# A decoder layer's compressed-value product, made from float32r parts instead of float32

## The chip, the cores and the metric

The kernel runs on one core of a Trainium2 chip. The metric is the device time of one execution, in microseconds (us); the median of the runs counts. Engines are named as in the profile: PE is the matrix engine (TensorE), PEld its weight load, DVE is VectorE, ACT is ScalarE, POOL is GpSimd, SP is the queue that issues most DMAs.

## The reference, cut to what matters

The layer takes 512 tokens of width 2048, makes one input projection, runs two mixers on it (a sparse attention and a gated spatial mixer), merges them, projects back and adds a gated per-layer embedding. The change touches one of the three branches of the attention: the compressed one. There, keys and values are compressed to 31 blocks for each of 4 groups, each group has 4 heads, and per query block:

```python
sc = jnp.einsum('bqgrd,bngd->bgrqn', qb, kc).astype(jnp.float32) * scale
sc = jnp.where(vc_mask, sc - slopes[:, :, None, None] * dc.astype(jnp.float32), NEG)
p_c = jax.nn.softmax(sc, axis=-1) * vc_mask
o_c = jnp.einsum('bgrqn,bngd->bqgrd', p_c.astype(vc.dtype), vc)
...
o = (gb[:, :, 0, :, :, None] * o_c + gb[:, :, 1, :, :, None] * o_s +
     gb[:, :, 2, :, :, None] * o_w)
```

The edited product is `o_c`: probabilities over compressed blocks (in the kernel already weighted by their gate) times compressed values. Everything is float32.

## The kernel before, in words

**Parts.** Nearly all large products are made of float32r parts. A float32 operand is split into a high part, rounded to float32r by a copy on ACT (`high`, line 141), and a low part, the remainder, made by a subtraction on DVE (`low`, line 147; with a scale, lines 143 and 149). A product is then three matmuls: high by high, high by low, low by high. The low part is often put off with `deferred`: a list of functions that `flush()` runs ahead of the next piece of PE work.

**Order.** The order of instructions is written out by hand. `gemm()` is a generator that yields after each small set of matmuls of the dense projections (lines 337 to 339 are those that run beside the attention: `ps_q` for queries, `ps_za` for the gate path); `fill(n)` advances it by n pieces. The attention phase, some 200 to 490 us in the profile, is a loop over 48 slots, six for each `ft`, a pair of heads. In each slot it issues events: `scores` (lines 999 and 1000, two heads), `weigh`, `transpose_probs` (line 1051), `values` (lines 1070 and 1071) and, at fixed slots, the pieces of the compressed branch. Behind each event that uses PE it runs `fill` for a share of the dense work.

**The compressed branch**, once for each of 4 groups g (each serves `ft` = 2g and 2g+1):
- `cmp_scores` (line 1103): eight float32r matmuls for four heads, 32 rows a head.
- `cmp_softmax`, `cmp_weigh`: transposes back to tokens, softmax pieces on DVE, ACT and POOL.
- `cmp_transpose` (lines 1142 to 1148): four transposes into one bank `ps_c`, so that the rows are 4 heads by 32 blocks and the columns are the 512 tokens; one copy on ACT takes the bank to the float32 tile `pct` (line 1144). POOL writes the values of the group into `vcb`, [128, 2, 128]: index 0 holds heads 0 and 1 in rows 0 to 63, index 1 heads 2 and 3 in rows 64 to 127, zeros elsewhere.
- `cmp_values(ft)` (line 1152): one float32 matmul, `vcb[:, ft % 2]` by `pct`. Half of the rows of the weights are zeros: they cancel the two heads that belong to the other `ft`. A copy on ACT brings the result to `oc` (line 1154).

For group 0 the first four pieces run ahead of the loop. For the later groups `cmp_transpose` comes in the fifth slot of `ft` = 2g, and `cmp_values` in the sixth slot of the even and the fourth of the odd `ft`.

**Banks.** The results of PE go to banks of 128 rows by 512 columns. Those of kind "s" are two, given out in turn (`bank("s", ...)`); scores of the two heads of a slot (`ps_s`) and all `ps_c` share them. A bank is given out again when all its readers are done. The tiles of the pool `att` work in the same way; each tag has as many slots as its `bufs`, and `pct`, `ct` and `oc` have one each.

Of the kernel before, what the change touches and what calls it, by code (L numbers as in the profile page):

```python
# [13 lines left out]
F32 = mybir.dt.float32  # L14
F32R = mybir.dt.float32r
BF16 = mybir.dt.bfloat16
AF = mybir.ActivationFunctionType
ALU = mybir.AluOpType
# [3 lines left out]
P = 128  # L22
S = 512
# [5 lines left out]
HD = 64  # L29
# [34 lines left out]
def kernel(ctx: ExitStack, tc: tile.TileContext, x, p, norm_g, w_in,  # L64
                      pe_k, w1_k, w2_k, pe_v, w1_v, w2_v, ln_g, ln_b, sgu_w, sgu_b,
                      w_up_a, w_up_b, w_out, w_ple, w_ple_gate, final_g, out):
    nc = tc.nc
    x, out = x[0], out[0]
    p = p[0, 0]
# [10 lines left out]
    def bank(kind, name):  # L80
        return psum.tile([P, 512], F32, tag=kind, name=name)
# [49 lines left out]
    deferred = []  # L131
# [7 lines left out]
    def high(hi, src, scale=None):  # L139
        if scale is None:  # L140
            nc.scalar.copy(hi, src)  # L141
        else:
            nc.scalar.mul(hi, src, scale)

    def low(hi, lo, src, scale=None):
        if scale is None:
            nc.vector.tensor_tensor(out=lo, in0=src, in1=hi.bitcast(F32), op=ALU.subtract)  # L147
        else:
            nc.vector.scalar_tensor_tensor(out=lo, in0=src, scalar=scale, in1=hi.bitcast(F32),
                                           op0=ALU.mult, op1=ALU.subtract)  # L150
# [639 lines left out]
    with tc.tile_pool(name="xin", bufs=4, side="right") as xin:  # L790
# [43 lines left out]
        for j in range(2):  # L834
            b = bank("t", "ps_p")
# [6 lines left out]
        b = bank("o", "ps_g")  # L842
# [41 lines left out]
    vc = mid.tile([P, GROUPS, HD], F32, name="vc")  # L884
# [18 lines left out]
    with tc.tile_pool(name="cmp", bufs=1) as cmp:  # L903
# [17 lines left out]
        for n in range(2):  # L921
            b = bank("t", "ps_pe")
# [25 lines left out]
        t = o32[:, 4, 128:256].rearrange("p (g n) -> p g n", g=GROUPS)  # L948
        h = o32[:, 5].rearrange("p (g r n) -> p g r n", g=GROUPS, r=4)
        c = cmp.tile([P, 1], F32, name="hid_c")  # L950
# [12 lines left out]
        b = bank("o", "ps_kc")  # L963
        nc.tensor.matmul(b[:, :128], w2t[lo_r].rearrange("e i f -> e (i f)"), h[lo_r, :, 0], start=True, stop=True)
        split(kc_h, kc_l, b[:, :128].rearrange("p (g n) -> p g n", g=GROUPS))
        b = bank("o", "ps_vc")
        for g in range(GROUPS):
            nc.tensor.matmul(b[:, g * HD:g * HD + HD], h[up_r, g].rearrange("e r n -> e (r n)"), w2t[up_r, 0],
                             start=True, stop=True)
# [5 lines left out]
    att = ph_b.enter_context(tc.tile_pool(name="att", bufs=1))  # L975
    tmp_pool.update(p=att, n=1)
    kcp = att.tile([P, 2, 224], F32R, name="kcp")
    vcb = att.tile([P, 2, P], F32, name="vcb")
    nc.gpsimd.memset(kcp.bitcast(F32), 0.0)
    nc.gpsimd.memset(vcb, 0.0)  # L980

    slots = []
    for ft in range(8):
# [1 line left out]
    prob, obank, oc_t, pct_t = {}, {}, {}, {}  # L985
# [152 lines left out]
    def cmp_transpose(g):  # L1138
        c, _ = pct_t["c"]
        b = bank("s", "ps_c")  # L1140
        for i in range(TT):
            nc.tensor.transpose(b[:, i * P:i * P + P], c[:, i].rearrange("p r n -> p (r n)"), ident)
        t = att.tile([P, S], F32, tag="pct", name="pct")
        nc.scalar.copy(t, b)
        pct_t["p"] = t
        for r in range(4):
            nc.gpsimd.tensor_copy(vcb[32 * r:32 * r + 32, r // 2, (r % 2) * HD:(r % 2) * HD + HD],
                                  vc[32 * r:32 * r + 32, g])

    def cmp_values(ft):  # L1150
        b = bank("s", "ps_c")
        nc.tensor.matmul(b, vcb[:, ft % 2], pct_t["p"], start=True, stop=True)
        t = att.tile([P, S], F32, tag="oc", name="oc")
        nc.scalar.copy(t, b)
        oc_t[ft] = t
# [3 lines left out]
    for f, u in zip((cmp_scores, cmp_softmax, cmp_weigh, cmp_transpose), (4, 3, 4, 8)):  # L1159
        fill(u)  # L1160
        flush()
        f(0)
    n = len(slots)
    credit, per_period = 0.0, (phase_b_units - 19) / (n + 3)
    for s in range(n + 3):
        events = []
        if s < n:
            ft, j = slots[s][0], s % 6
            events.append((scores, s))
        if 1 <= s <= n:  # L1170
            events.append((weigh, s - 1))
        tq = [(transpose_probs, s - 2, bi) for bi in range(len(blocks(s - 2)))] if 2 <= s <= n + 1 else []
        vq = [(values, s - 3, bi) for bi in range(len(blocks(s - 3)))] if s >= 3 else []
        events += tq[:1] + vq[:1]
        if s < n:
            if ft % 2 == 1 and ft < 7 and j == 3:
                events.append((cmp_keys, (ft + 1) // 2))
            if ft % 2 == 1 and ft < 7 and j == 5:
                events.append((cmp_scores, (ft + 1) // 2))
            if ft % 2 == 0 and ft > 0 and j in (1, 2, 4):  # L1180
                events.append(({1: cmp_softmax, 2: cmp_weigh, 4: cmp_transpose}[j], ft // 2))
            if j == (3 if ft % 2 else 5):
                events.append((cmp_values, ft))
        events += tq[1:] + vq[1:]
        share = per_period / sum(e[0] not in off_pe for e in events)
        for e in events:
            if e[0] not in off_pe:
                flush()
            e[0](*e[1:])
            if e[0] not in off_pe:  # L1190
                credit += share
                fill(int(credit))
                credit -= int(credit)
# [134 lines left out]
    b = bank("s", "ps_b")  # L1328
# [3 lines left out]
    for hf in range(2):  # L1332
        b = bank("s", "ps_w")
        for j in range(4):
            nc.tensor.transpose(b[:, j * P:j * P + P], wn[hf][:, j], ident)
        nc.vector.tensor_tensor(out=ws[hf], in0=b.rearrange("p (g t) -> p g t", g=4),
                                in1=tri.unsqueeze(1).to_broadcast([P, 4, P]), op=ALU.mult)
# [386 lines left out]
```

## Time and profile before

| | |
|---|---|
| median of 3 runs | 1564.4 us (1564.28 to 1564.46) |
| profiled execution | 1564.27 us |
| its span | 1562.6 us |
| PE busy | 1548.0 us, 99% of the span |
| DVE busy | 1162.8 us, 74% |
| ACT busy | 772.7 us, 49% |
| POOL busy | 223.8 us, 14% |
| `cmp_values` matmuls (line 1152) | 16 records for 8 calls, 591 ns each, from 245.4 to 465.7 us |
| copies `pct` (line 1144) | 4, 576 ns each, at 220.0, 309.0, 375.6 and 441.1 us |

The span is the time from the first to the last instruction in the trace; the execution's own time lies a little above it. A row of the timeline gives start, duration, engine, line, operation, output and inputs, and in brackets for how long the engine stood idle before and what released it. Matmuls are pipelined: one starts before the one ahead has ended, so the distance between starts is what one costs.

### The profile page before, as it was taken

Reading aid. Unit: us, or ns where it says so; the run is one execution under the profiler, and the core shown is the slowest. Engines: PE = TensorE matmul, PEld = TensorE weight load, DVE = VectorE, ACT = ScalarE, POOL = GpSimd, SP = SyncE. Lnnn points to the kernel's source line nnn. Section 1 sums busy time; section 2 is a strip of 40 time slices with the busy share of each in tenths; the row PEclk is TensorE's granted clock in tenths of the full one; section 3 lists DMA queues with packets and bytes.
Section 4 is the critical chain, followed back from the end, with each engine's and each line's share of the span. In section 5 each row is a group of like instructions: output and inputs, shape, how many; then the busy total and the mean of one; then the engine's idle time right before and its main releaser. Section 6 shows DMA issues by size and latency. Waiting matters only on the chain.

```text
span 1562.6 us, 20467 instructions
## 1 busy us (share of the span) xinstructions
PE 1548.0 (99%) x7486; PEld 1296.4 (83%) x7486; DVE 1162.8 (74%) x1851; ACT 772.7 (49%) x1337; POOL 223.8 (14%) x348
## 2 busy tenths in 40 slices
PE   9999999999999999999999999999999999999997
PEld 8889988888888888888888888888888888888885
DVE  6543358888886977878887777777656587888877
ACT  6433346667664544454544444444423343544556
POOL 1200000101022520101121211220122221000000
PEclk9999999999999999999999999999999999999999
DMA  9423421112123993617473736675742387464654
GB/s 325 123 81 87 114 78 45 51 45 55 41 55 109 288 293 93 215 54 242 134 265 103 270 100 243 208 261 208 262 156 84 125 259 246 148 201 164 188 206 185
DMA packets 158213, 250.35 MB, mean 160 GB/s; under 512 B 8713, under 2 KB 82081, under 8 KB 156065
## 3 DMA queue, kind: packets, MB, share of 16 engines
q1 hardware_dynamic: 116224, 150.10, 31.0%
q0 software_dynamic: 41744, 98.69, 19.0%
q8 instruction: 59, 0.97, 0.3%
q14 instruction: 42, 0.34, 0.1%
q10 hardware_dynamic: 144, 0.26, 0.0%
HBM read 199.21 MB, written 49.81 MB: 159 GB/s over the span
## 4 chain that ended last, share of the span: by engine, by line
PE 96%; DVE 2%; ACT 1%; issue 0%; POOL 0%; DVEq 0%; POOLq 0%; ACTq 0%
PE ps_m L311 7%; PE ps_m L313 7%; PE ps_m L312 7%; PE ps_za L337 2%; PE ps_za L339 2%; PE ps_t L1051 2%; PE ps_za L338 2%; PE ps_u L349 2%; PE ps_u L350 2%; PE ps_ub L351 2%; PE ps_wo L349 2%; PE ps_ub L349 2%; PE ps_ub L350 2%; PE ps_wo L350 2%; PE ps_wo L351 2%; PE ps_u L351 2%
## 5 line engine op out<-in xcount | busy, mean ns | idle before, releaser
L147 DVE TENSOR_TENSOR ls<-b,hs 128x1024 fp32r<-128x1024 f32 x180 | 220.2, 1224 | 119.3 <-ACT hs L141 118.4
L141 ACT CAST hs<-b 128x1024 fp32r<-128x1024 f32 x180 | 189.2, 1052 | 213.4 <-PE ps_m L313 86.1
L147 DVE TENSOR_TENSOR lo<-raw,hi 128x512 fp32r<-128x512 f32 (+1 forms) x248 | 173.0, 703 | 111.3 <-issue 27.2
L141 ACT CAST hi<-raw 128x512 fp32r<-128x512 f32 (+1 forms) x248 | 149.5, 608 | 187.9 <-PE ps_ub L351 46.4
L141 ACT CAST hs<-raw 128x1024 fp32r<-128x1024 f32 x72 | 75.8, 1053 | 88.8 <-PE ps_m L313 35.8
L147 DVE TENSOR_TENSOR ls<-raw,hs 128x1024 fp32r<-128x1024 f32 x72 | 88.0, 1222 | 16.8 <-ACT hs L141 16.7
L311 PE MATMUL ps_m<-hs,act_h 128*128 128x512 f32 x256 | 100.5, 393 | 0.0
L312 PE MATMUL ps_m<-ls,act_h 128*128 128x512 f32 x256 | 99.7, 389 | 0.0
L313 PE MATMUL ps_m<-hs,act_l 128*128 128x512 f32 x256 | 99.7, 389 | 0.0
L240 DVE TENSOR_TENSOR b<-b,b 128x1024 f32<-128x1024 f32 x72 | 87.7, 1218 | 0.0
L240 DVE TENSOR_TENSOR b<-raw,b 128x1024 f32<-128x1024 f32 x72 | 87.6, 1217 | 0.0
L141 ACT CAST pth<-ps_t 128x512 fp32r<-128x512 f32 (+1 forms) x88 | 47.9, 545 | 65.7 <-PE ps_t L1051 65.4
L1012 ACT ACTIVATE prob<-prob,st 128x512 f32<-128x512 f32 (+3 forms) x128 | 70.6, 555 | 4.0 <-DVE st L1003 3.8
L147 DVE TENSOR_TENSOR ptl<-ps_t,pth 128x512 fp32r<-128x512 f32 (+1 forms) x88 | 56.2, 638 | 21.1 <-ACT pth L141 20.3
L1003 DVE CUSTOM_DVE_ANT_0 prob<-ps_s,b 128x512 f32<-128x512 f32 (+3 forms) x128 | 56.3, 486 | 10.1 <-PE ps_s L1000 9.9
L313 PEld LDWEIGHTS ps_m<-hs,act_l 128*128 128x128 f32 x256 | 48.0, 188 | 10.1
L311 PEld LDWEIGHTS ps_m<-hs,act_h 128*128 128x128 f32 x256 | 48.1, 188 | 9.7
L312 PEld LDWEIGHTS ps_m<-ls,act_h 128*128 128x128 f32 x256 | 48.1, 188 | 9.7
L337 PE MATMUL ps_za<-act_h,hi 128*128 128x512 f32 x128 | 55.8, 436 | 0.0
L337 PE MATMUL ps_q<-act_h,hi 128*128 128x512 f32 x128 | 53.6, 419 | 0.0
L1051 PEld LDWEIGHTS ps_t<-ident,prob 128*128 128x128 f32 x320 | 39.7, 140 | 13.9 <-DVE ptl L147 2.8
L1051 PE MATMUL ps_t<-ident,prob 128*128 128x128 f32 x320 | 49.5, 273 | 1.3 <-DVE ptl L147 1.2
(590 smaller groups left out, 4374.3 us busy)
## 6 DMA issues: line engine op xcount, KB each, us to landing
raw<-in_w_in_dram SPq DMA_DIRECT2D x116, 512.0 KB, 3.9
b<-in_w_in_dram SPq DMA_DIRECT2D x48, 512.0 KB, 5.4
raw<-in_w_out_dram SPq DMA_DIRECT2D x24, 512.0 KB, 4.7
raw<-in_w_ple_gate_dram SPq DMA_DIRECT2D x24, 512.0 KB, 4.1
raw<-in_w_up_b_dram SPq DMA_DIRECT2D x16, 512.0 KB, 3.9
oa_d<-oa POOLq DMA_DIRECT2D x28, 256.0 KB, 4.7
gate<-keep POOLq DMA_DIRECT2D x24, 256.0 KB, 3.7
xt<-in_x_dram SPq DMA_DIRECT2D x4, 1024.0 KB, 10.3
```

Source lines behind the costliest of these rows:

```text
L141: nc.scalar.copy(hi, src)
L147: nc.vector.tensor_tensor(out=lo, in0=src, in1=hi.bitcast(F32), op=ALU.subtract)
L240: nc.vector.tensor_tensor(out=b[o], in0=b[x], in1=b[y], op=ALU.subtract)
L311: nc.tensor.matmul(o, ah, hi[:, i], start=st, stop=False, skip_group_check=go)
L312: nc.tensor.matmul(o, ah, lo[:, i], start=False, stop=False, skip_group_check=go)
L313: nc.tensor.matmul(o, al, hi[:, i], start=False, stop=sp, skip_group_check=go)
L337: nc.tensor.matmul(ps, hi[:, j], ah, start=st, stop=False)
L349: nc.tensor.matmul(o, ah[:, sl], hi[:, j], start=st, stop=False)
L350: nc.tensor.matmul(o, ah[:, sl], lo[:, j], start=False, stop=False)
L351: nc.tensor.matmul(o, al[:, sl], hi[:, j], start=False, stop=sp)
L1012: nc.scalar.activation(sl, sl, AF.Exp, bias=st[:, 0, j, hh:hh + 1], scale=-1.0, accum_out=st[:, 1, j, hh:hh + 1])
L1051: nc.tensor.transpose(b[:, (2 * e + hh) * P:(2 * e + hh + 1) * P], pts[hh][:, c:c + P], ident)
```

## The change

`vcb` and the probabilities become float32r. `vcb` index 0 now holds the high parts of the values for all four heads, index 1 their low parts. The probabilities are kept in two tiles, one for each `ft` of the group: in the tile for the even `ft`, rows 0 to 63 hold the high parts of heads 0 and 1, and rows 64 to 127, which met zeros before, hold the low parts of the same two heads; in the tile for the odd `ft` it is the other way round, for heads 2 and 3. A matmul by index 0 so gives high values times (high + low) probabilities, and one by index 1 low values times the same; both add up in one bank.

The copy of the bank on ACT becomes two copies of 64 rows each. Two subtractions of 64 rows on DVE, which read the bank and the high parts, are put in `deferred`. POOL makes a subtraction behind each of its four copies into `vcb`. The second tile takes the slot `ct`. Each fp32 matmul of `cmp_values` becomes two float32r matmuls.

```diff
-    vcb = att.tile([P, 2, P], F32, name="vcb")
+    vcb = att.tile([P, 2, P], F32R, name="vcb")
     nc.gpsimd.memset(kcp.bitcast(F32), 0.0)
-    nc.gpsimd.memset(vcb, 0.0)
+    nc.gpsimd.memset(vcb.bitcast(F32), 0.0)
...
         for i in range(TT):
             nc.tensor.transpose(b[:, i * P:i * P + P], c[:, i].rearrange("p r n -> p (r n)"), ident)
-        t = att.tile([P, S], F32, tag="pct", name="pct")
-        nc.scalar.copy(t, b)
-        pct_t["p"] = t
+        rows = slice(0, 64), slice(64, 128)
+        pct_t["p"] = [att.tile([P, S], F32R, tag=tag, name="p" + tag) for tag in ("pct", "ct")]
+        for e, t in enumerate(pct_t["p"]):
+            high(t[rows[e]], b[rows[e]])
+
+        def lows():
+            for e, t in enumerate(pct_t["p"]):
+                low(t[rows[e]], t[rows[1 - e]], b[rows[e]])
+        deferred.append(lows)
         for r in range(4):
-            nc.gpsimd.tensor_copy(vcb[32 * r:32 * r + 32, r // 2, (r % 2) * HD:(r % 2) * HD + HD],
-                                  vc[32 * r:32 * r + 32, g])
+            rw, c = slice(32 * r, 32 * r + 32), slice((r % 2) * HD, (r % 2) * HD + HD)
+            nc.gpsimd.tensor_copy(vcb[rw, 0, c], vc[rw, g])
+            nc.gpsimd.tensor_tensor(out=vcb[rw, 1, c], in0=vc[rw, g], in1=vcb[rw, 0, c].bitcast(F32), op=ALU.subtract)
 
     def cmp_values(ft):
         b = bank("s", "ps_c")
-        nc.tensor.matmul(b, vcb[:, ft % 2], pct_t["p"], start=True, stop=True)
+        for j in range(2):
+            nc.tensor.matmul(b, vcb[:, j], pct_t["p"][ft % 2], start=j == 0, stop=j == 1)
         t = att.tile([P, S], F32, tag="oc", name="oc")
```

## The prediction

> **What bounds the kernel now.** I read the page's first and fourth part, then the waits of PE, then the busy time of the stretch that holds the edited work.
>
> ```profile
> span 1562.6 us, 20467 instructions
> ...
> PE 1548.0 (99%) x7486; PEld 1296.4 (83%) x7486; DVE 1162.8 (74%) x1851; ACT 772.7 (49%) x1337; POOL 223.8 (14%) x348
> ...
> PE 96%; DVE 2%; ACT 1%; issue 0%; POOL 0%; DVEq 0%; POOLq 0%; ACTq 0%
> ```
> ```profile
> PE ps_spin L812 <- POOL eps_t L86: 1.4, 1, 1.4
> PE ps_t L1051 <- DVE ptl L147: 1.2, 1, 1.2
> PE ps_pl L345 <- ACT hi L141: 0.7, 1, 0.7
> PE ps_s L999 <- ACT pct L1144: 0.2, 1, 0.2
> ```
> ```profile
> 280.00:310.00 30.00, 28.66 (x165) 24.14 (x164) 26.54 (x73) 19.59 (x52) 5.45 (x10) 1.00 0.14 36
> ...
> 200.00:480.00 280.00, 278.30 (x1544) 234.36 (x1543) 231.36 (x688) 179.33 (x482) 32.60 (x58) 1.00 0.20 52
> ```
>
> PE is busy for 99% of the span and holds 96% of the chain, and these four waits (waiter and line, releaser, total, times, longest) are all that it has for other engines in the whole span, two at the start and two in the attention phase. So PE time is program time: a microsecond that PE saves, or one that it stands idle, moves the end by a microsecond, as nothing after the attention phase lies in wait to swallow it. In the attention phase (200 to 480 us, where all edits lie) PE is busy for 278.30 of 280 us, at a granted clock of 1.00. DVE is second there, at 231.36 us, and in one of its densest stretches (280 to 310 us) 26.54 of 30. One of PE's two waits in this phase, a score matmul (L999) that waits for the copy `pct` (L1144), is for a line that is edited.
>
> **Term 1: the fp32 product becomes two float32r products.**
>
> ```profile
> L1152 PE MATMUL ps_c<-pct,vcb x16: 590/591/592, 245.4 to 465.7; 128*128 128x512 f32 x16
> ```
> ```profile
> 312.66 1.02 PE L1152 MATMUL ps_c<-pct,vcb 128*128 128x512 f32 x2
> 313.12 0.79 PE L337 MATMUL ps_q<-act_h,hi 128*128 128x512 f32 x1
> 313.75 0.39 PE L338 MATMUL ps_q<-act_l,hi 128*128 128x512 f32 x1
> 313.98 0.40 PE L339 MATMUL ps_q<-act_h,lo 128*128 128x512 f32 x1
> ```
> ```profile
> 206.80 2.01 PE L1103 MATMUL ps_c<-qs,kcp 128*128 128x512 f32 x8
> 208.65 0.40 PE L337 MATMUL ps_za<-act_h,hi 128*128 128x512 f32 x1
> ```
>
> Matmuls overlap, so the price is the distance between starts, not the duration. The eight calls of `cmp_values` leave 16 records, two to a call. From the first start of the pair (312.66) to L338 (313.75) are 1.09 us, in which L337 also ran; L337 is worth one normal pitch, 313.98 - 313.75 = 0.23. The fp32 pair so takes 0.86. The nearest rows for what replaces it are the eight float32r products of `cmp_scores`, the same shape: 208.65 - 206.80 = 1.85 for eight, 0.231 each, 0.46 for two. Saved: 0.86 - 0.46 = 0.40 a call, times 8 = 3.2 us. All of it is PE time, so all of it counts.
>
> [...]
>
> **Term 2: the score bank is held longer.** Before, one copy on ACT (L1144) emptied the bank `ps_c` in each of the four `cmp_transpose` calls. Now ACT makes two 64-row copies (the highs), and then DVE reads the same bank twice (`lows`). Who waits: banks of kind "s" are two, handed out in turn. The scores of a slot take one each, `cmp_transpose` takes the first again, so the next slot's first score gets the other bank and its second score gets the one that `lows` still reads. In the built order of the changed kernel this second L999 waits for DVE, behind both subtractions. PE runs in order, so all that is queued behind L999 stands too.
>
> Prices of the new work, from the splits that have the same form (64x512 out of a bank, in pairs, the low part written to the other half of the rows):
>
> ```profile
> 235.02 1.19 ACT L143 ACTIVATE qs<-ps_q 64x512 fp32r<-64x512 f32 x2
> ...
> 236.24 1.39 DVE L149 SCALAR_TENSOR_TENSOR qs<-ps_q,qs 64x512 fp32r<-64x512 f32 x2 [0.45 <-ACT qs L143]
> ```
> A pair of half copies takes 1.19 on ACT; half the rows are not half the time. DVE begins 0.03 after the second copy (235.02 + 1.19 = 236.21, then 236.24), though its first subtraction needs the first copy alone; a pair of subtractions takes 1.39. The built order agrees for the new lines: the first subtraction waits for ACT, the second for no ACT event of its own, so the first wait covers both copies. From the start of the first copy to the release of the bank are therefore 1.19 + 0.03 + 1.39 = 2.61 us. Against that stand the times at which PE now starts the second score:
>
> ```profile
> 220.01 0.59 ACT L1144 COPY pct<-ps_c 128x512 f32<-128x512 f32 x1 [1.38 <-PE ps_c L1142]
> ...
> 220.65 0.51 PE L999 MATMUL ps_s<-ob_h,qs 128*128 128x512 f32 x1 [0.21 <-ACT pct L1144]
> 220.99 0.40 PE L1000 MATMUL ps_s<-ob_l,qs 128*128 128x512 f32 x1
> ```
> ```profile
> 308.48 0.68 DVE L147 TENSOR_TENSOR ptl<-ps_t,pth 128x512 fp32r<-128x512 f32 x1
> ...
> 309.00 0.58 ACT L1144 COPY pct<-ps_c 128x512 f32<-128x512 f32 x1
> ...
> 309.08 0.68 DVE L147 TENSOR_TENSOR lo<-raw,hi 128x512 fp32r<-128x512 f32 x1
> ...
> 310.11 0.28 PE L999 MATMUL ps_s<-ob_h,qs 128*128 128x256 f32 x1
> ```
> ```profile
> 375.58 0.57 ACT L1144 COPY pct<-ps_c 128x512 f32<-128x512 f32 x1
> ...
> 376.33 0.28 PE L999 MATMUL ps_s<-ob_h,qs 128*128 128x256 f32 x1
> ```
> ```profile
> 441.09 0.58 ACT L1144 COPY pct<-ps_c 128x512 f32<-128x512 f32 x1
> ...
> 441.81 0.30 PE L999 MATMUL ps_s<-ob_h,qs 128*128 128x256 f32 x1
> ```
>
> In group 0 the second L999 starts 0.05 after its bank is free (220.01 + 0.59 = 220.60, then 220.65), so release to start is 0.05 and the whole delay 2.66. Group 0: 220.01 + 2.66 = 222.67, late by 2.02. Group 1: 311.66 against 310.11, late by 1.55. Group 2: 378.24 against 376.33, 1.91. Group 3: 443.75 against 441.81, 1.94. Together 7.4 us in which PE stands. The row of group 0 shows this wait already at work, at 0.21 us. It also shows the price of starting again: from 220.65 to 220.99 are 0.34 instead of 0.23, so 0.1 more for each of the three groups that had no wait before: 0.3. 0.23 is the pitch of term 1. Term 2 is 7.7 us lost. These prices are already those without any overlap inside a pair, so I take them as the upper end; the lower end is the first rival's.
>
> **What I cost at nothing.** ACT gains one copy a group (0.6 us, four times) and is busy for 179 of 280 us here; `pth` behind it comes 0.6 later, but its user is then held by the stall of 1.6 to 2 us. DVE gains 5.6 us in all. Its next work, the score reductions, starts in group 1 after the subtractions and one short `ptl`, about 1.7 us late, and PE is late by as much, so the order of arrival stays. POOL doubles its `vcb` work:
>
> ```profile
> 301.94 1.23 POOL L1147 COPY vcb<-vc 32x64 f32<-32x64 f32 x4
> ```
>
> Four more small operations of 0.3 end near 304.5, and the product that needs them starts at 312.66: 8 us of cover; without it each call would wait for some 1.2 us. The odd half of the probabilities now stands in the slot `ct`, which the next group's scores take over two slots after its last product. No DMA is issued or moved.
>
> **Sum.** 7.7 - 3.2 = 4.5 us slower. The profiled execution took 1564.27 us around its span of 1562.6; the median of the runs is 1564.4, 0.1 above, which is nothing here. 1564.3 + 4.5 = 1568.8. The measurement can tell about 0.2% (3.1 us) from no change, and 4.5 is 0.29%.
>
> **The rivals.**
>
> *First, the subtractions follow copy by copy.* Each subtraction waits for its own half only and is pipelined like the full-height ones (308.48, then 309.08: 0.60 apart). Then group 0 has 220.01 + 0.59 + 0.03 + 0.60 + 0.69 + 0.05 = 221.97, late by 1.32; group 1, where DVE is not free before 309.08 + 0.60 = 309.68, 309.68 + 0.60 + 0.69 + 0.05 = 311.02, late by 0.91; groups 2 and 3, by the sum of group 0, 1.2 each. That is 4.6, with 0.3 for starting again 4.9, less 3.2: 1.7 slower, 1566.0, within what counts as the same. For it: the halves are different rows. Against it: the pair at 235.02 was waited for to its end, and the built order has one ACT wait. [...] 12%.
>
> *Second, the bank is free in time, and only the saving is left.* If the second score did not meet this bank, or both subtractions ended before it is due (in group 1 within 1.1 us of the first copy's start), the time would be 1564.3 - 3.2 = 1561.1, faster by just 0.2%. Against it stands the 0.21 us for which L999 already waits for `pct`: the bank is the one, and there is no slack in group 0. 5%.
>
> *Third, DVE knocks on.* In its dense stretches it is 88% busy, and L1051 has already waited 1.2 for it once. If the transposes after each stall find no slack, PE's earlier arrival by 0.40 after each product, with some 0.1 by which DVE is later than PE, comes back as waits: 0.5 in three groups, 1.5 in all, 1570.3. 13%.
>
> *Fourth, the two new products do not run at the float32r pitch* and the pair still takes 0.86: then 7.7 slower, 1572.0. Against it are the eight rows of `cmp_scores`, with the same kinds of operands. 4%.
>
> **How the numbers follow.** The forecast has 62%, and 4% is left for cases that I do not see. Forecast, third and fourth rival are slower by over 0.2%: 0.62 + 0.13 + 0.04 = 0.79. The first rival and the unseen cases make 0.16 within it, the second rival 0.05 faster. The range reaches down to the first rival and up past the third, 1565.8 to 1570.8; the second, the fourth and the unseen stay outside, 13% together.
>
> **What the profile after would show.** Right: PE waits at L999 for DVE at the `lows` line, four times, 1.5 to 2.1 each, near 7.4 us together; L1144's rows replaced by pairs of 1.2 on ACT and of 1.4 on DVE; the value products at 0.46 from start to start of the next work; no other new wait of PE over half a microsecond. I am wrong if the four waits are near one microsecond (first rival), if they are missing (second), if L1051 waits in several places (third), or if the products keep 0.86 (fourth).

## The result, and the profile after

The changed kernel takes 1575.6 us (median of 5 runs, 1572.45 to 1575.89), against 1564.4 before (1564.28 to 1565.27): 1.0065 times as long, interval 1.0055 to 1.0076. It is 11.2 us slower where 4.5 were forecast; the sign was right, the size was not, and the range was missed. The profiled execution took 1575.69 us, so it is a usual one.

The first and fourth part of the page of the changed kernel, then all its waits of PE (waiter and line, releaser, total us, times, longest):

```profile
span 1573.7 us, 20498 instructions
...
PE 1551.3 (99%) x7486; PEld 1300.5 (83%) x7486; DVE 1169.0 (74%) x1859; ACT 775.4 (49%) x1341; POOL 228.8 (15%) x364
...
PE 95%; DVE 3%; ACT 2%; issue 0%; POOL 0%; DVEq 0%; ACTq 0%; POOLq 0%
```
```profile
PE ps_s L999 <- DVE pct L147: 7.6, 4, 2.3
PE ps_t L1051 <- DVE ptl L147: 1.6, 2, 1.3
PE ps_spin L812 <- POOL eps_t L86: 1.4, 1, 1.4
PE ps_pl L345 <- ACT hi L141: 0.3, 1, 0.3
PE ps_c L1142 <- DVE st L1003: 0.2, 1, 0.2
```

The foretold wait is there, four times, 7.6 us in all, and L1051 waits 0.4 more than before. But PE's busy time should have gone down by the 3.2 us that the products save, and it went up by 3.3 (1548.0 to 1551.3). PE stands longer *and* works longer. The timeline of group 0 shows why:

```profile
220.14 0.58 ACT L141 CAST ppct<-ps_c 64x512 fp32r<-64x512 f32 x1 [1.38 <-PE ps_c L1142]
...
220.74 0.58 ACT L141 CAST pct<-ps_c 64x512 fp32r<-64x512 f32 x1
221.35 0.68 DVE L147 TENSOR_TENSOR ppct<-ps_c,ppct 64x512 fp32r<-64x512 f32 x1 [1.71 <-ACT pct L141]
222.07 0.69 DVE L147 TENSOR_TENSOR pct<-ps_c,pct 64x512 fp32r<-64x512 f32 x1
...
222.91 0.76 PE L999 MATMUL ps_s<-ob_h,qs 128*128 128x512 f32 x1 [2.34 <-DVE pct L147]
...
223.90 0.63 PE L337 MATMUL ps_q<-act_h,hi 128*128 128x512 f32 x1
...
224.32 0.63 PE L338 MATMUL ps_q<-act_l,hi 128*128 128x512 f32 x1
...
226.29 0.40 PE L337 MATMUL ps_q<-act_h,hi 128*128 128x512 f32 x1
...
226.53 0.40 PE L338 MATMUL ps_q<-act_l,hi 128*128 128x512 f32 x1
```

The two copies on ACT, then the two subtractions on DVE, then L999 after 2.34 us of standing. Behind that wait the matmuls start 0.42 to 0.43 apart (223.90, 224.32); from 226.29 on they start 0.24 apart, close to the usual 0.23. The other three restarts:

```profile
314.78 0.36 PE L999 MATMUL ps_s<-ob_h,qs 128*128 128x256 f32 x1 [1.50 <-DVE pct L147]
...
382.75 0.36 PE L999 MATMUL ps_s<-ob_h,qs 128*128 128x256 f32 x1 [1.86 <-DVE pct L147]
...
451.30 0.49 PE L999 MATMUL ps_s<-ob_h,qs 128*128 128x256 f32 x1 [1.85 <-DVE pct L147]
```

And windows of the same trace (stretch, its length, busy time of PE, PEld, DVE, ACT and POOL; the third column from the end is the granted clock):

```profile
222.67:226.08 3.41, 3.17 (x8) 2.52 (x9) 2.15 (x6) 1.09 (x2) 0.00 (x0) 0.50 0.00 0
...
315.00:320.00 5.00, 5.00 (x30) 4.22 (x30) 3.60 (x18) 3.39 (x12) 0.00 (x0) 1.00 0.21 61
...
383.10:386.50 3.40, 3.40 (x15) 2.91 (x14) 2.63 (x15) 1.05 (x4) 0.00 (x0) 0.50 0.27 80
...
451.36:454.77 3.41, 3.41 (x11) 2.85 (x12) 2.57 (x15) 0.54 (x2) 0.00 (x0) 0.50 0.37 111
```

Behind the waits of 2.34, 1.86 and 1.85 us the granted clock is one half for 3.4 us; behind the wait of 1.50 it is 1.00. I call such a stretch at half the clock a dip. PE is "busy" through it, which is why its busy time rose. By an estimate from these rows, 3.4 us of work at a pitch of 0.43 instead of 0.23 hold 3.4 x (1 - 0.23/0.43) = 1.6 us of loss.

To see where each microsecond goes I set the start of the same PE instruction in two traces side by side. The table is worked out from the traces: start in the named kernel less start before, in us, at chosen points of the time before. The last three columns are experiments, described below. A hold is the stretch in which PE stands because the bank is still being read (its cost in the table has in it the slow stretch behind), and a product is one call of `cmp_values`.

| at (before) | what lies ahead of it | changed | e3 (dummies) | e1 (one copy) | e9 (POOL) |
|---|---|---|---|---|---|
| 215 | start | 0.13 | -0.34 | -0.03 | 0.10 |
| 229 | hold, group 0 | 3.78 | 1.79 | -0.04 | 0.10 |
| 300 | 2 products | 2.94 | 0.97 | -0.85 | -0.74 |
| 320 | hold 1, 1 product | 4.37 | 2.36 | -1.04 | -1.08 |
| 365 | 1 product | 3.98 | 1.98 | -1.44 | -1.46 |
| 371 | | 4.39 | 2.39 | -1.04 | -1.33 |
| 384 | hold 2, 1 product | 7.65 | 4.08 | -0.97 | -1.65 |
| 436 | 1 product | 7.29 | 3.69 | -1.34 | -2.02 |
| 448 | hold 3, 1 product | 10.74 | 5.60 | -1.08 | -2.30 |
| 480 | 1 product | 10.36 | 5.20 | -1.47 | -2.68 |
| 1545 | the rest of the program | 10.68 | 5.22 | -1.38 | -2.28 |

Each product moves PE forward by about 0.39. With that taken out, the four holds cost the changed kernel 3.65, 1.75, 3.65 and 3.84 us (the second is taken from 306 us on, where the column stands at 3.01). The second is the one without a dip. Nearly all of the loss arises in the attention phase; the thousand microseconds behind it add 0.3.

### The profile page after: what moved, and what is told of

Its sections match the earlier page's. It is cut to its first block, busy times and chain, and to the rows that moved or that the text cites. A ratio compares the mean times of both kernels' runs of the same rounds, so it can differ in the third digit from the quotient of the medians.

```text
span 1573.7 us, 20498 instructions
## 1 busy us (share of the span) xinstructions
PE 1551.3 (99%) x7486; PEld 1300.5 (83%) x7486; DVE 1169.0 (74%) x1859; ACT 775.4 (49%) x1341; POOL 228.8 (15%) x364
## 4 chain that ended last, share of the span: by engine, by line
PE 95%; DVE 3%; ACT 2%; issue 0%; POOL 0%; DVEq 0%; ACTq 0%; POOLq 0%
PE ps_m L311 6%; PE ps_m L312 6%; PE ps_m L313 6%; PE ps_u L349 2%; PE ps_u L351 2%; PE ps_ub L351 2%; PE ps_wo L350 2%; PE ps_ub L349 2%; PE ps_ub L350 2%; PE ps_wo L351 2%; PE ps_wo L349 2%; PE ps_u L350 2%; PE ps_t L1051 2%; PE ps_za L337 2%; PE ps_za L339 2%; PE ps_za L338 2%
## 5 line engine op out<-in xcount | busy, mean ns | idle before, releaser
L1051 PE MATMUL ps_t<-ident,prob 128*128 128x128 f32 x320 | 50.4, 277 | 1.7 <-DVE ptl L147 1.6
L1051 PEld LDWEIGHTS ps_t<-ident,prob 128*128 128x128 f32 x320 | 40.4, 142 | 14.0 <-DVE ptl L147 3.3
```

The source lines that it names most:

```text
L1051: nc.tensor.transpose(b[:, (2 * e + hh) * P:(2 * e + hh + 1) * P], pts[hh][:, c:c + P], ident)
```

## The experiments

The theory: the loss hangs on the bank that is held, partly as standing time and partly as the half clock behind it, and the clock falls when PE has stood for long enough. Against it: the time lies in the added work of DVE and ACT and stays when bank or clock are spared; or the clock has another cause. `e1` to `e4` were run beside one another, then `e5` to `e7`, then `e8` to `e10`; "before" is the median of the kernel before on the same chip.

### One copy out of the bank, the parts made from it

```diff
+        raw_c = att.tile([P, S], F32, tag="oc", name="rawc")
+        nc.scalar.copy(raw_c, b)
...
-            high(t[rows[e]], b[rows[e]])
+            high(t[rows[e]], raw_c[rows[e]])
...
-                low(t[rows[e]], t[rows[1 - e]], b[rows[e]])
+                low(t[rows[e]], t[rows[1 - e]], raw_c[rows[e]])
```

> Edit: one ACT copy takes the bank ps_c to a float32 tile in the slot oc, as before the change; highs and lows read that tile, so the bank is free after 0.6 us. The product stays two float32r matmuls. Theory A (PE stands idle for the bank, 7.6 us, and each idle time of 1.8 us or more also halves the granted clock for some 3.4 us, about 1.6 us lost three times): no L999 wait over 0.2 us, clock 1.00 from 200 to 480 us, time 1564.4 - 3.2 = 1561.2 us (1560.5 to 1562.5). Rival B (the 6.5 us beyond waits and saving come from DVE and ACT having more to do): ACT has even more to do here, DVE as much, so only the waits go: 1575.6 - 7.6 = 1568 us.

Measured: 1564.04 us (10 runs), before 1564.66; ratio 0.9996, interval 0.9987 to 1.0006. Its waits of PE, and a window of group 2:

```profile
PE ps_t L1051 <- DVE ptl L147: 1.6, 2, 1.3
...
PE ps_c L1162 <- DVE st L1003: 0.4, 2, 0.2
...
PE ps_s L999 <- ACT rawc L1146: 0.2, 1, 0.2
```
```profile
385.00:390.00 5.00, 5.00 (x28) 4.21 (x27) 3.91 (x12) 3.87 (x9) 0.74 (x1) 1.00 0.43 108
```

The waits behind the subtractions and the dips are gone, so the hold of the bank is the cause of the whole loss: 11.5 us lie between this kernel and the changed one, for an extra copy on ACT. But it is 2.8 us over the time expected of the theory: not the 3.1 us of the products are kept but 1.47 at 480 us. The table shows where it is given back: between 365 and 371, and around the products of groups 2 and 3, where PE waits for DVE.

### Useful work in the gap

The changed kernel with three pieces of dense work put between the two heads' scores in the four slots concerned, taken off the work behind that slot:

```diff
+    gaps, spent = {0, 17, 29, 41}, [0]
...
+            if hh and s in gaps:
+                fill(3)
+                spent[0] += 3
...
-                credit += share
-                fill(int(credit))
-                credit -= int(credit)
+                credit += share - spent[0]
+                spent[0] = 0
+                todo = max(0, int(credit))
+                fill(todo)
+                credit -= todo
```

> Edit: the change as it is, but in the slot behind each cmp_transpose three pieces of the dense projection (nine matmuls, 2.1 us) are taken from later in the slot and set between the first and the second head's score, so that PE has work while the bank is held. Theory A: waits at L999 fall from 7.6 to under 1 us, no clock drop, 1561 to 1562.5 us. Rival B: DVE and ACT have the same work as in the changed kernel, so about 1568 us.

Measured: 1564.54 us (10 runs), before 1564.66; ratio 0.9999, interval 0.9989 to 1.0008. The window of group 0, and the one wait for the subtractions that is left:

```profile
220.00:225.00 5.00, 4.70 (x21) 3.30 (x20) 3.41 (x8) 2.78 (x6) 1.30 (x5) 1.00 0.07 22
```
```profile
PE ps_s L1003 <- DVE pct L147: 0.3, 1, 0.3
```

The bank is held as long as in the changed kernel, by the same copies and subtractions (in group 0 for 2.63 us, from 220.21 to 222.84, there for 2.62, from 220.14 to 222.76); PE just has other work in that time, and both the standing and the half clock are gone. The loss was PE's waiting and what follows from it, not the added work as such. Here too most of the saving is missing.

### Useless work in the gap

Five matmuls of 128x512 ahead of the first score in the same slots, into the bank that the score then overwrites. They cost PE time, but shorten its standing:

```diff
+            for _ in range(5 if hh == 0 and s in (0, 17, 29, 41) else 0):
+                nc.tensor.matmul(b, q, ob_h[:, s0], start=True, stop=True)
```

> Edit: the change, with five useless matmuls (128x512, 1.16 us) ahead of the first score in the four slots behind cmp_transpose; their results are overwritten. The bank is free as late as before, so PE reaches the second score at the same time, but stands idle for 0.35 to 1.2 us instead of 1.5 to 2.34. Theory A: the granted clock stays at 1.00 and three times some 1.6 us come back: 1575.6 - 4.8 = 1570.8 us (1570 to 1571.8). Rival B: nothing changes, 1575.6 us.

Measured: 1570.84 us (4 runs), before 1564.66; ratio 1.0042, interval 1.0027 to 1.0057. The waits that are left, and the windows of groups 0 and 2:

```profile
PE ps_s L1001 <- DVE pct L147: 2.9, 4, 1.2
```
```profile
220.00:225.00 5.00, 3.83 (x17) 2.84 (x16) 3.46 (x7) 2.18 (x6) 0.87 (x3) 1.00 0.01 2
...
380.00:385.00 5.00, 4.31 (x27) 3.70 (x27) 4.46 (x18) 2.57 (x11) 0.00 (x0) 1.00 0.37 103
```

Twenty matmuls that compute nothing made the kernel 4.7 us faster. PE reaches the work behind the hold no earlier for them, so all of that is the clock. By the table the holds cost 2.13, 1.71, 2.08 and 2.30 here, against 3.65, 1.75, 3.65 and 3.84: 1.5, 0, 1.6 and 1.5 less, 4.7 together, and nothing where there was no dip before.

The same with two dummies instead of five leaves one wait about as long as the shortest behind which the changed kernel has a dip, 1.85 us:

> Edit: e3 with two useless matmuls instead of five: PE idles for 1.9, 1.0, 1.4 and 1.4 us behind the four cmp_transposes. Theory A (idle times up to 1.78 us left the clock alone in every trace so far, from 2.10 on all halved it, between them it went both ways): at most one dip, 1570.8 us without it and 1572.4 with it. If idle time of 1.4 us were enough: three dips, 1575.6 us.

Measured: 1571.36 us (4 runs), 1570.9 to 1572.84; before 1564.7, ratio 1.0043, interval 1.0029 to 1.0057. The profile is of the run of 1572.84, and has one dip, behind the longest of its waits (1.87); behind 1.04, 1.39 and 1.39 there is none (1.00 from 315 to 320, 385 to 390 and 450 to 455 us). The window behind the first:

```profile
225.00:230.00 5.00, 5.00 (x17) 3.96 (x16) 1.60 (x6) 1.79 (x5) 0.00 (x0) 0.70 0.40 105
```

The other three runs lie 1.4 to 1.9 below, as without that dip. They have no profile, but the record gives the mean granted clock of each run: 0.998 for these three, 0.996 for the profiled one. Of the twelve traces of this case, the seven without a dip have a mean of 0.997 or 0.998 and the five with one of 0.995 or 0.996, so these three runs had no dip as far as the mean can tell.

### The hold alone

This starts from the kernel before: its fp32 product is kept, and with it its `vcb`; the bank is copied in two halves and read by two subtractions into a tile that nobody uses:

```diff
-        nc.scalar.copy(t, b)
+        spare = att.tile([P, S], F32R, tag="ct", name="spare")
+        rows = slice(0, 64), slice(64, 128)
+        for e in range(2):
+            nc.scalar.copy(t[rows[e]], b[rows[e]])
+
+        def lows():
+            for e in range(2):
+                nc.vector.tensor_tensor(out=spare[rows[1 - e]], in0=b[rows[e]], in1=t[rows[e]], op=ALU.subtract)
+        deferred.append(lows)
```

> Edit: the kernel before with its fp32 product, but the bank is copied in two halves and read by two DVE subtractions (into a spare tile that nobody uses), as in the change. Both theories: the loss without the saving, 1575.6 + 3.2 = 1578.8 us. If the float32r product saved nothing: 1575.6 us. If the hold cost less than the trace says: below 1575.

Measured: 1575.57 us (4 runs), before 1564.66; ratio 1.0069, interval 1.0052 to 1.0086. That is 3.2 under the expectation. The two last holds, then the window that ends inside the wait of 1.88, the one behind that, and the one behind the wait of 1.93:

```profile
384.31 0.36 PE L999 MATMUL ps_s<-ob_h,qs 128*128 128x256 f32 x1 [1.88 <-DVE spare L1151]
...
451.94 0.36 PE L999 MATMUL ps_s<-ob_h,qs 128*128 128x256 f32 x1 [1.93 <-DVE spare L1151]
```
```profile
380.54:383.95 3.41, 1.90 (x13) 1.45 (x11) 2.90 (x6) 2.51 (x7) 0.00 (x0) 1.00 0.12 18
383.96:387.36 3.40, 3.05 (x17) 2.53 (x18) 3.30 (x17) 1.35 (x6) 0.00 (x0) 1.00 0.46 135
...
452.23:455.63 3.40, 3.40 (x12) 2.80 (x11) 2.57 (x16) 0.93 (x4) 0.00 (x0) 0.50 0.24 73
```

It stands for 7.7 us, like the changed kernel, but this run has two dips and not three: 1.88 passed without one, 1.85 in the changed kernel did not. So the expectation was wrong in taking the number of dips for fixed. PE is 12.3 us late at 1545 in this profile (of a run of 1576.72); one more dip would make the 13.8 that the sum asks for (10.7 of the changed kernel and the 3.1 of its products). The median is 1.2 lower still. The other three runs have no profile; their mean granted clock is 0.998 (1574.04 us) and 0.997 (1575.75 and 1575.4), against 0.996 in the profiled one, which fits fewer dips in each of them. The time is the 1575.6 that the expectation gave for a float32r product that saves nothing, but that reading is out: the products start 0.46 apart in the changed kernel, and each moves PE forward by 0.39 in the table.

### A ladder of holds

The kernel before, with 2, 5, 3 and 8 extra copies of the bank on ACT in the four groups, into a tile that nobody uses:

```diff
+        spare = att.tile([P, S], F32, tag="ct", name="spare")
+        for _ in range((2, 5, 3, 8)[g]):
+            nc.scalar.copy(spare, b)
```

> Edit: the kernel before, with 2, 5, 3 and 8 useless further copies of the bank on ACT in groups 0 to 3, so that PE's second score waits for some 1.2, 2.0, 1.4 and 3.9 us. Read only the granted clock behind each wait. Theory A (an idle time of about 1.8 us or more halves the clock for some 3.4 us, one of 1.5 us or less does not): dips behind groups 1 and 3 alone, each about as long, whatever the idle time was. Rival (the dip needs a full window of idle time, about as long as the dip itself, 3.4 us): a dip in group 3 alone; the dips of the changed kernel would then be something else.

Measured: 1579.04 us (one run), before 1564.85. The three longest waits and the windows behind them (the first group waits 0.8):

```profile
313.67 0.48 PE L999 MATMUL ps_s<-ob_h,qs 128*128 128x256 f32 x1 [2.31 <-ACT spare L1147]
...
383.15 0.39 PE L999 MATMUL ps_s<-ob_h,qs 128*128 128x256 f32 x1 [1.43 <-ACT spare L1147]
...
453.66 0.53 PE L999 MATMUL ps_s<-ob_h,qs 128*128 128x256 f32 x1 [4.54 <-ACT spare L1147]
```
```profile
315.00:320.00 5.00, 5.00 (x23) 3.96 (x22) 2.87 (x10) 3.25 (x12) 0.00 (x0) 0.78 0.01 2
...
385.00:390.00 5.00, 5.00 (x25) 3.82 (x24) 3.58 (x10) 3.21 (x12) 0.00 (x0) 1.00 0.00 0
...
455.00:460.00 5.00, 5.00 (x22) 3.82 (x21) 2.87 (x10) 3.30 (x12) 0.00 (x0) 0.78 0.00 0
```

No float32r product, no subtraction and no DVE here, and the dips are the same. So they belong to PE's standing, whatever holds it. After 1.43 us there is none; after 2.31 and after 4.54 there is one each, of the same size (0.78 in both windows). A dip lasts as long after twice the wait. That is the theory's forecast; the rival had a dip behind the last wait alone.

### Where the saving went when the bank is free

`e1` keeps half of the products' saving. Two causes were open: DVE's queue, which got 5.6 us of subtractions, or the place of the product right behind them. Four variants of `e1` tell them apart. In the first, the subtractions go to POOL, and the product of the even `ft` comes at the end of its slot:

```diff
+        for e, t in enumerate(pct_t["p"]):
+            nc.gpsimd.tensor_tensor(out=t[rows[1 - e]], in0=raw_c[rows[e]], in1=t[rows[e]].bitcast(F32), op=ALU.subtract)
...
-            if j == (3 if ft % 2 else 5):
+            if j == 3 and ft % 2:
...
+        if s < n and j == 5 and ft % 2 == 0:
+            events.append((cmp_values, ft))
```

> Edit: as in e1, but the low parts of the probabilities are made by POOL from the float32 copy instead of DVE, and the product for the even ft stands at the end of its slot instead of in the middle, so that POOL has time. Theory (in e1 and e2 the saving of 3.2 us was given back by DVE, whose 5.6 us more delay the score reductions, so that products and transposes wait for a bank): without DVE work more of it stays, 1564.6 - 3.2 + 0.3 = 1561.7 us. Rival (the saving is not there, or the waits come from the order of instructions): 1564 as in e1.

Measured: 1562.99 us (11 runs), before 1564.85; ratio 0.9986, interval 0.9977 to 0.9995. That lies between the theory (1561.7) and the rival (1564), and the edit changes two things at once; the third and fourth variant part them.

In the second, DVE keeps the subtractions, but one slot later, in the slot of the product, which again comes at its end (`events.append((lambda g: pct_t["lows"](), ft // 2))` in place of `deferred.append(lows)`):

> Edit: as in e1, with the same subtractions on DVE, but issued one slot later (in the slot of the product, when DVE has idle time) and the product for the even ft at the end of its slot. Theory: DVE has its 5.6 us more, but not in the queue ahead of the score reductions: between e1 and e6, 1562 to 1563 us. If DVE's load as such is what costs: 1564 as in e1.

Measured: 1572.56 us (5 runs), before 1564.85; ratio 1.0045, interval 1.0033 to 1.0058. A clear miss, by 10 us:

```profile
315.86 0.70 PE L1162 MATMUL ps_c<-ppct,vcb 128*128 128x512 f32 x2 [2.10 <-DVE ppct L147]
...
385.93 0.69 PE L1162 MATMUL ps_c<-ppct,vcb 128*128 128x512 f32 x2 [1.75 <-DVE ppct L147]
...
453.16 0.70 PE L1162 MATMUL ps_c<-ppct,vcb 128*128 128x512 f32 x2 [1.78 <-DVE ppct L147]
```

Now the product waits, 5.8 us in four waits, because the subtractions stand in DVE's queue behind the work of that slot (in group 1 the first starts at 315.02, right behind a `lo` of 314.33). Only the wait of 2.10 has a dip behind it (a clock of 0.57 from 316 to 320 us).

The third is `e1` with nothing but the product at the end of the slot, the fourth is `e1` with the subtractions on POOL and the product in its old place:

> Edit: e1 (one copy of the bank, lows on DVE from it) with the product for the even ft at the end of its slot. Parts e6 in two. Theory (DVE's queue gives back part of the saving): still near e1, 1563.5 to 1564.5 us. If it was the place of the product in the slot that counted: as e6, 1563.0 us.

Measured: 1563.92 us (11 runs), before 1564.7; ratio 0.9993, interval 0.9984 to 1.0002.

> Edit: e1 with lows on POOL and the product in its old place. If DVE's queue is what counts: about 1563 us, or somewhat more where POOL's two subtractions are not done when the product is due (they start 1.2 us after the copy and take some 0.7 each, the product is due 3.5 us after the copy). If the place counts: 1564 us.

Measured: 1562.55 us (11 runs, 1561.74 to 1563.23), before 1564.7; ratio 0.9985, interval 0.9976 to 0.9994. Its longest wait of PE in the attention phase, and the work for the even half in group 1:

```profile
PE ps_t L1051 <- DVE ptl L147: 1.3, 1, 1.3
```
```profile
309.71 1.28 POOL L1155 TENSOR_TENSOR ppct<-rawc,ppct 64x512 fp32r<-64x512 f32 x1 [5.74 <-PE ps_s L1000]
...
311.97 0.62 PE L1160 MATMUL ps_c<-ppct,vcb 128*128 128x512 f32 x2
```

The place makes no difference that these runs can tell (`e8` against `e1`: 1563.92 and 1564.04, on two chips; `e9` against `e6`: 1562.55 and 1562.99). The engine does: on one chip, `e8` with the subtractions on DVE runs from 1563.15 to 1564.78, `e9` with them on POOL from 1561.74 to 1563.23. POOL takes 1.28 us for a subtraction (0.7 was expected) where DVE takes 0.69, but POOL has the time: the even half is ready at 310.99 (309.71 + 1.28), and its product starts at 311.97. `e9` keeps 2.8 of the 3.1 us up to 480, and is faster than both kernels: 2.15 us under the kernel before, 13 under the changed one.

## Why the prediction was wrong, and what in it was right

**Term 1 was right.** In the changed kernel the product and the work behind it start 0.46 apart, as forecast:

```profile
386.93 0.62 PE L1160 MATMUL ps_c<-ppct,vcb 128*128 128x512 f32 x2
387.39 0.39 PE L337 MATMUL ps_q<-act_h,hi 128*128 128x512 f32 x1
```

The alignment gives about 0.39 for each of eight calls, 3.1 us of a forecast 3.2. The fourth rival is out.

**The stall in term 2 was right.** Four waits of L999 for the second subtraction, 2.34, 1.50, 1.86 and 1.85, against 2.02, 1.55, 1.91 and 1.94 by which PE was to be late (in group 0 with 0.21 of waiting before): 7.3 net, forecast 7.4. The first rival is out: the first subtraction waited for both copies in each group. The second rival is out.

**The step that failed is the price of starting again, in term 2.** I read it off the one restart that the trace before had, behind 0.21 us of standing, 0.1 us, and carried it to waits ten times as long: 0.3 in all. Behind three of the four waits PE came back at half the clock for 3.4 us, which cost 1.5 to 1.6 us each, 4.7 in all. `e3` shows this size, with and without the dips; `e5` shows that standing alone does it. I had looked at the clock only as 1.00 over the phase and taken it as given. The trace before holds no wait in this phase that would show a dip: its longest, 1.2 us, is one of those after which no trace here shows one. So the price was unknown there, and a range that bounds unknown costs should have had room for it.

**Which waits are followed by a dip.** A wait's length alone does not say: the hold-only run has a wait of 1.88 us without a dip, the changed kernel one of 1.85 with one. The traces give the rest. In each of them all changes of the granted clock lie a whole number of 3.413 us apart: in the changed kernel it falls at 222.67, 383.09 and 451.36 us, 47 and then 20 times that, and it rises 3.413 us after each fall. So the time can be cut into stretches of 3.413 us by these points, and what sets the slow ones apart in these traces is how long PE was busy in the stretch before each. One stretch of the changed kernel, then two of `e7`, which come one behind the other:

```profile
379.68:383.09 3.41, 1.55 (x11) 1.24 (x10) 2.89 (x6) 1.83 (x4) 0.00 (x0) 1.00 0.33 73
```
```profile
449.65:453.06 3.41, 1.73 (x10) 1.11 (x8) 3.29 (x11) 1.84 (x8) 0.00 (x0) 1.00 0.08 25
453.07:456.47 3.40, 3.05 (x14) 2.29 (x15) 2.83 (x9) 0.59 (x1) 0.00 (x0) 1.00 0.00 0
```

The first holds the whole wait of 1.86, PE is busy for 1.55 us of it, and the next stretch runs at 0.50 (383.10:386.50, above). In the second PE is busy for 1.73 us, and the next one stays at 1.00. Over the twelve traces, start and end of the program aside, PE is busy for at most 1.56 us in the nine stretches ahead of a dip, and for at least 1.73 us in every other stretch. The wait of 1.50 lies whole in one stretch, 311.42 to 314.83, and leaves PE busy for 1.91 us of it; the next one stays at 1.00. The wait of 1.88 in `e4` lay across the border at 383.95 (382.44 to 384.31), so that PE was still busy for 1.90 us of the stretch before it. Where the borders fall against the program differs from trace to trace, so the number of dips would differ between runs of one kernel, as the mean clocks of the four runs with two dummies say it does (0.996 and 0.998). This rule was found in the traces afterwards; no run was made to test it by moving a wait.

**Two smaller sizes.** Without the clock the holds cost 8.2 us (`e3`), not 7.7, which the prediction took for the upper end. And the third rival's mechanism is there in part: 0.4 us are lost between 365 and 371 us, where L1051 waits for DVE's `ptl`, and 0.1 between 300 and 306; the rival had 1.5. The sum by the runs: 8.2 + 4.7 + 0.5 - 3.1 = 10.3, against 10.36 in the table at 480 us.

**What I cost at nothing** cost nothing in this kernel, the 0.5 us behind DVE aside. But for DVE the cover was the stall itself, as the prediction has it, and `e1` against `e9` prices what is under it: with the bank free, DVE's 5.6 us cost PE 1.2 us up to 480 (2.68 - 1.47), while POOL carries the same work for nothing.

**Open.** Four runs of the changed kernel lie within 0.8 us; the fifth took 1572.45, 3.1 below the median. Two dips fewer would explain it. It has no profile; its mean granted clock is 0.996 where the profiled run with three dips has 0.995, which fits fewer dips, but the run of 1575.14 has 0.996 too, so the record cannot count them.

## What to carry to other kernels

A wait of a busy matrix engine is not priced by its length alone: see whether it can make the clock fall (here, whether it left PE busy for no more than 1.56 us of one stretch of 3.41 us; at 1.73 the clock stayed), and if it can, add the slow stretch behind it; to fill the gap, even partly, can be worth more than the time filled (`e10` took the four waits from 7.6 to 5.7 us and the kernel from 1575.6 to 1571.4). Take a result out of a shared bank with one copy and make the parts from that copy, since here the further readers of the bank held up the matmul that got it next, by 7.6 us in all where one copy left 0.2. And give added work to the engine with the slack, even if it is slower there: here POOL took nearly twice as long as DVE for each subtraction (1.28 us against 0.69), and the kernel was faster for it (`e9` 1562.55 us, `e8` 1563.92).

## What the runs showed of the hardware that was not expected

- **The clock.** Over all the traces of this case, in the attention phase: after the waits looked at from 1.39 to 1.78 us (1.39 twice, 1.43, 1.50, 1.53, 1.75, 1.78) no dip; at 1.85, 1.86, 1.87 and 1.93 a dip and at 1.88 none; at 2.10, 2.31, 2.34, 2.37 and 4.54 a dip each time. What parts them is the busy time of PE in one stretch of 3.413 us between two of the clock's borders: at most 1.56 us in those that a dip follows, at least 1.73 in all others. A dip lasted 3.41 us at half the clock, behind waits from 1.85 to 4.54 us.
- **Half the rows, the whole time.** A copy of 64x512 took ACT 0.58 us, like one of 128x512 (0.58). The subtractions of 64x512 took 0.68 and 0.69 on DVE, like those of 128x512 (0.68 before, at 308.48 and 309.08), and began 0.72 apart (221.35, 222.07) where those two of full height began 0.60 apart: the second half did not start before the first had ended (221.35 + 0.68 = 222.03). In one stretch of `e7` both stand side by side: two of full height start at 313.73 and 314.33, the two halves at 315.02 and 315.74. What makes the difference no run here tried by itself.
- **In this kernel two readers of a bank go one after the other; two readers of a tile do not.** The rows show the waits that the program as built has. From the bank, DVE's first subtraction began 0.03 after ACT's *second* copy had ended (220.74 + 0.58 = 221.32, then 221.35, above). From the tile `rawc` of `e1`, it began 0.03 after its own half was ready, while ACT was at work on the other:

```profile
308.85 0.62 ACT L141 CAST ppct<-rawc 64x512 fp32r<-64x512 f32 x1
...
309.50 0.62 ACT L141 CAST pct<-rawc 64x512 fp32r<-64x512 f32 x1
309.50 0.69 DVE L147 TENSOR_TENSOR ppct<-rawc,ppct 64x512 fp32r<-64x512 f32 x1 [0.51 <-ACT ppct L141]
```
